# A decoder trunk on one core: u's tiles split in portions, merge factors spread together, roots spread later, two more final tiles beside VectorE

## The chip, the cores and the metric

The kernel runs on one core of a Trainium2 chip. The metric is the device time of one execution in microseconds (us). The time before is 2108.82 us, the median of three runs (2108.45 to 2113.14). The profile is one more execution of its own, which took 2107.84 us.

## The reference

A trunk of two layers over 1024 positions of width 1024, all in fp32. Each layer is a mixer and a dense MLP, both with RMS norm ahead and a residual add behind. The first mixer is a spatial gate, the second a dilated attention in three groups of heads. Cut to what matters:

```python
def rms_norm(x, g):
    return x * rsqrt(mean(x * x, -1) + EPS) * g

def chunk_gating_mixer(h, ...):                 # layer 0
    u, v = split(gelu(h @ w_in), 2)
    v = layer_norm(v, ln_g, ln_b)
    mixed = einsum('gts,bnsgc->bntgc', tril(w_s), v) + b_s
    return (u * mixed) @ w_out

def dilated_attention_mixer(h, ...):            # layer 1
    for g, (window, dil) in enumerate(((128, 1), (512, 4), (2048, 16))):
        num[g], den[g], m[g] = dilated_group(q[g], k[g], v[g], rel_bias)
    scale = [exp(m[g] - max(m)) for g in range(3)]
    return (sum(num * scale) / sum(den * scale)) @ w_out

for layer in range(2):
    h = h + mixer(rms_norm(h, mix_g))
    h = h + relu(rms_norm(h, mlp_g) @ w_up) ** 2 @ w_down
return rms_norm(h, final_g)
```

## The kernel before

**Layout and precision.** The residual stream h lies transposed in SBUF, 8 tiles of 128 features by 1024 positions. A half is 512 positions. Every fp32 product is made of three passes in a rounded fp32 type: an operand is split into hi, a copy that ScalarE makes (L226), and lo = x - hi, which VectorE makes (L227), and TensorE multiplies hi by hi, hi by lo and lo by hi into one bank (`mm`, L198). A tile of eight k is so 24 matmuls of 128x512.

**What sets the order.** TensorE's order is the order of the code. Beside the main line run generators on a modelled clock: `flow.add(gen, after)` puts one in the list, and the main line's `flow.pump()` advances those whose time has come; `yield ns` puts a generator off by that much modelled time. So a number in `flow.add` or `yield` says between which matmuls of the main line a generator's instructions stand. The other engines' orders follow from the same program by a scheduler that works with priorities; `tc.high_priority` lifts an instruction, `tc.issue_after(x)` keeps what stands in it behind the instruction x. Each engine then runs its own list strictly in that order.

**Banks.** The eight PSUM banks are two pools: three banks called mm and five called at. A product waits until the bank that its tile was given has been read out.

**Mixer 0.** `v` is made first, in three groups of chunks (`gi` 0, 1, 2) of up to six banks each. ScalarE's Gelus (L731) empty them, with 1/rms of the positions as scale. That root is found behind a group's last products (`sq[gi].rms`), and `spread_rms` (a generator) spreads it over 128 partitions: four transposes of `rs` on TensorE (L205, at<-ident,rs) and ScalarE's copy to `rsb`. The gate's weights give row sums by two matmuls a half (at<-wsh,tr and at<-wsl,tr), read by VectorE at L683. Then `u` is made: 16 tiles, eight m by two halves s, in groups of m (0, 1, 2), (3), (4), (5, 6, 7). `u_out` empties a tile: VectorE multiplies by `rsb` into a temp (L790), ScalarE takes the Gelu (L791), VectorE multiplies four chunks of v in place (L794). When a half's last tile is out, `u_split(s)` splits all eight m of it for the product with w_o: four hi copies (ScalarE) and four lo (VectorE, y<-vg,y) of 128x128 per m. Numbered in their order, tile 14 is (s = 1, m = 5), 15 is (1, 6), 16 is (1, 7). Beside that, `prepare` makes sums of w_qkv's blocks for a seven-product scheme, splits them (tr) and stores them by SyncE's queue (wd<-tr), which also carries the loads.

**Attention.** `merge(hp, i)` joins the three groups' results for a pair of heads hp and a half i. It makes factors f of 128x3x4x2, and for g = 1, 2 and then 0: `factors(g)` copies them out to 128x512 (ScalarE), `spread_factors` transposes that on TensorE into an at bank, and VectorE multiplies the numerators by it (L1694 for g = 1, 2). Between g's it yields modelled time, so that matmuls of the main line stand between.

**The end.** The last norm is done by `final` for a half and for the quarters 2 and 3 (columns 512 to 767 and 768 to 1023): the root (L256 to L265), its spread, then eight tiles h x g x pb by VectorE (L1878), stored in pairs of k by SyncE (outT<-t). In quarter 3 the pair k = 4, 5 goes another way (`ASIDE`): ScalarE copies pb (L1869) and makes h x g (L1875), GpSimd multiplies (L1876).

Of the kernel before, what the change touches and what calls it, by code (L numbers as in the profile page):

```python
# [31 lines left out]
def half(s):  # L32
    return slice(s * HALF, (s + 1) * HALF)


def blk(b, n=1):
    return slice(b * P, (b + n) * P)
# [80 lines left out]
BESIDE = (8, 9, 10)  # L118
STEPS = (5, 3)
ROOTS = ((0, 7, 0, 1, 0), (1, 7, 0, 1, 2))  # L120
GATE, ROWS, RB = 6, 10000, 5
NARROW = 68
ASIDE = {768: (4,)}
EARLY = 4
PACE = (1700.0, 1800.0, 3000.0)
LAT = dict(sum=2600.0, rms=2600.0, tile=1600.0, gate=8500.0, soft=5500.0, turn=4200.0, fe=1300.0, v=2000.0, qk=4200.0, merge=2600.0, out=700.0, fex=3.0, ve=1600.0, vd=6000.0, ex=18000.0, ones=900.0)
# [3 lines left out]
def trunk(ctx: ExitStack, tc: tile.TileContext, xT, w_u, w_v, w_o, w_s, b_s, w_qkv, w_vt, w_bo, rel,  # L130
# [524 lines left out]
    def spread_rms(s):  # L655
        pb = spread(rs[:, 4 * s:4 * s + 4])
        nc.scalar.activation(rsb[:, half(s)], pb, AF.Copy)
        yield 0
# [76 lines left out]
    for gi, chunks in enumerate(((0, 1, 2), (3, 4, 5), (6, 7))):  # L735
        banks = {}
        for k in range(KT):
# [35 lines left out]
            for e, i, n, f in order:  # L773
                x, c = ys[n // 4][k], blk(n % 4)
                matmul(banks[n, f], x[e == 1][:, c], w[e == 2][:, half(f)], start=(k == 0 and e == 0),
                       stop=(k == 7 and e == 2))
                if e == 2:
                    flow.pump()
                if (gi, k, i, f, e) in ROOTS:
                    for _ in sq[gi].sums():  # L780
                        pass
                    sq[gi].rms(rs[:, 4 * gi:4 * gi + 4])
                    flow.add(spread_rms(gi), 4000)
                if k == 7 and e == 2 and f == 1 and (i or gi == 2):
                    v_out(banks, chunks[:i + 1])

    def u_out(m, s, ps):
        t = temp()
        with tc.high_priority(offset=PRIO):
            nc.vector.tensor_tensor(t, ps, rsb[:, half(s)], op=ALU.mult)  # L790
        nc.scalar.activation(t, t, AF.Gelu)  # L791
        for b in range(4):
            x = vg[4 * s + b][:, blk(m)]
            nc.vector.tensor_tensor(x, x, t[:, blk(b)], op=ALU.mult)  # L794

    def u_split(s):
        out = []
        for m in range(8):
            hi, lo = pair().both()
            for b in range(4):  # L800
                split(hi[:, blk(b)], lo[:, blk(b)], vg[4 * s + b][:, blk(m)])
            out.append((hi, lo))
        return out

    us = []
    for tiles in ((0, 1, 2), (3,), (4,), (5, 6, 7)):
        w = [weight(w_u[m]) for m in tiles]
        if tiles[0] == 3:
            flow.add(prepare(PREPARED[0], PACE[0]))
        for s in range(2):  # L810
            for i, m in enumerate(tiles):
                b = mm_bank()
                mm(b, w[i], KCOLS, ys[s])
                flow.until(lambda: gated[4 * s + 3].t is not None)
                u_out(m, s, b)
            if tiles[-1] == 7:
                us.append(u_split(s))


    sq = [Square(half(0)), Square(half(1))]  # L820
# [821 lines left out]
    def merge(hp, i):  # L1642
# [38 lines left out]

        rest = None
        fe_ns = LAT["fe"] * (2.2 if hp == 3 else LAT["fex"])
        for g in (1, 2):
            fe = factors(g)
            if g == 2 and hp == 3:
                mine = factors(0)
            yield fe_ns
            if hp < 3:
                yield from turn_for(CALM[3])  # L1690
            pb = spread_factors(fe)
            t = temp()
            with tc.issue_after(whole[hp, 0]) if hp == 3 and (hp, 0) in whole else nullcontext():
                nc.vector.tensor_tensor(own(t, g), permuted(us_[g].N, i, g), own(pb, g), op=ALU.mult)  # L1694
            if rest is None:
                rest = t
            else:
                nc.vector.tensor_tensor(rest, rest, t, op=ALU.add)
# [258 lines left out]
```

## Time and profile before

| | us |
|---|---|
| median of 3 runs | 2108.82 |
| lowest, highest | 2108.45, 2113.14 |
| profiled execution | 2107.84 |
| its span | 2106.1 |
| outside the span | 1.74 |
| TensorE busy in the span | 2083.1 |

The granted TensorE clock is 0.998. The profile's page gives busy time by engine and the chain that ended last; the trace gives what each engine waited for, and rows of instructions in order of time. Such a row is: start, duration, engine, line, operation, output<-inputs, shapes, count, and in brackets the idle time before it with what ended it. Rows of several instructions merge neighbours of one kind, and neighbouring instructions overlap a little, so a pitch is a difference of starts rather than a duration.

### The profile page before, as it was taken

What the parts mean: (1) busy time and instruction counts of PE and PEld (TensorE: products, weight loads), DVE (VectorE), ACT (ScalarE), POOL (GpSimd) and SP (SyncE); (2) the same over time, 40 slices, a digit from 0 to 9 for tenths busy, and PEclk for the clock granted to TensorE, in tenths of its full rate; (3) what the DMA queues carried; (4) which work ended last, traced back from release to release, by engine and by line L of the source; (5) the groups of instructions that cost most, each with busy time, mean ns of one, the idle gap of its engine ahead of it and who ended that gap; (6) DMA issues with size and microseconds to landing.
All of it is one profiled execution on the core that took longest, in us unless ns stands there. A gap on an engine that the chain in (4) does not pass through costs nothing.

```text
span 2106.1 us, 30736 instructions
## 1 busy us (share of the span) xinstructions
PE 2083.1 (99%) x10160; PEld 1720.9 (82%) x10160; DVE 1572.8 (75%) x2902; ACT 1183.3 (56%) x2387; POOL 498.7 (24%) x368
## 2 busy tenths in 40 slices
PE   9999999999999999999999999999999999999998
PEld 7888888888888888888888788888888888888887
DVE  7878759766689998887746666757985446987776
ACT  7645435566675555435556666776556556544432
POOL 3000124323324333430000000002432222433244
PEclk9999999999999999999999999999999999999999
DMA  6428813688766767644865656482256443655432
GB/s 221 130 91 297 308 36 135 200 278 271 261 221 195 230 213 226 233 160 151 307 208 154 184 163 187 156 271 80 91 196 204 146 152 131 203 163 163 141 115 80
DMA packets 224756, 387.10 MB, mean 184 GB/s; under 512 B 39897, under 2 KB 67668, under 8 KB 224596
## 3 DMA queue, kind: packets, MB, share of 16 engines
q1 hardware_dynamic: 215456, 383.77, 55.4%
q10 hardware_dynamic: 9140, 1.36, 0.4%
q8 instruction: 80, 1.31, 0.3%
q14 instruction: 80, 0.66, 0.1%
HBM read 252.24 MB, written 132.81 MB: 183 GB/s over the span
## 4 chain that ended last, share of the span: by engine, by line
PE 84%; DVE 8%; DMA 2%; ACT 2%; issue 2%; POOL 1%; SPq 0%; DVEq 0%; POOLq 0%; ACTq 0%
PE mm L198 42%; PE at L198 40%; PE at L205 2%; DVE y L227 1%; DVE t L227 1%; DVE tr L227 1%; DMA t<-in_w_qkv 1%; DMA h<-in_xT 1%; DVE wp L227 0%; DVE q L1438 0%; DVE r L444 0%; DVE hx L227 0%; DMA r<-in_w_v 0%; POOL t L284 0%; DVE b L449 0%
## 5 line engine op out<-in xcount | busy, mean ns | idle before, releaser
L227 DVE TENSOR_TENSOR wp<-r,wp 128x512 fp32r<-128x512 f32 (+3 forms) x399 | 324.7, 819 | 124.4 <-ACT wp L226 122.1
L226 ACT ACTIVATE wp<-r 128x512 fp32r<-128x512 f32 (+3 forms) x399 | 236.2, 597 | 317.2 <-PE at L198 195.4
L198 PE MATMUL mm<-t,wp 128*128 128x512 f32 x1368 | 344.8, 395 | 0.0
L198 PE MATMUL at<-hx,wp 128*128 128x512 f32 x1452 | 341.0, 389 | 1.7 <-DVE h L1080 1.6
L198 PEld LDWEIGHTS at<-hx,wp 128*128 128x128 f32 x1452 | 272.1, 188 | 60.0 <-DVE h L1080 3.1
L198 PEld LDWEIGHTS mm<-t,wp 128*128 128x128 f32 x1368 | 250.7, 188 | 52.9 <-issue 0.7
L284 POOL TENSOR_TENSOR t<-t 128x512 f32<-128x512 f32 (+1 forms) x60 | 76.8, 1281 | 801.7 <-ACT t L279 799.7
L198 PE MATMUL at<-y,wp 128*128 128x512 f32 x1008 | 245.3, 389 | 0.0
L198 PE MATMUL mm<-hx,wp 128*128 128x512 f32 x984 | 234.3, 389 | 0.0
L198 PEld LDWEIGHTS at<-y,wp 128*128 128x128 f32 x1008 | 189.0, 188 | 39.6 <-issue 0.4
L198 PEld LDWEIGHTS mm<-hx,wp 128*128 128x128 f32 x984 | 184.5, 188 | 38.7 <-DVE hx L227 0.2
L198 PE MATMUL mm<-y,wp 128*128 128x512 f32 x816 | 209.8, 396 | 1.1 <-DVE y L227 0.6
L382 POOL TENSOR_TENSOR t<-r 128x512 f32<-128x512 f32 (+3 forms) x62 | 85.0, 1372 | 476.3 <-DMA r<-in_w_up 146.4
L198 PEld LDWEIGHTS mm<-y,wp 128*128 128x128 f32 x816 | 149.2, 188 | 33.0 <-DVE y L227 1.1
L227 DVE TENSOR_TENSOR hx<-t,hx 128x512 fp32r<-128x512 f32 x192 | 158.7, 831 | 6.1 <-ACT hx L226 5.6
L198 PE MATMUL mm<-y,whi 128*128 128x512 f32 x512 | 158.3, 390 | 1.1 <-DVE t L790 1.1
L198 PE MATMUL at<-t,wp 128*128 128x512 f32 x552 | 130.6, 389 | 0.0
L226 ACT ACTIVATE hx<-t 128x512 fp32r<-128x512 f32 x192 | 119.1, 628 | 19.9 <-DMA t<-hid 16.0
L384 POOL TENSOR_TENSOR r<-r 128x512 f32<-128x512 f32 (+3 forms) x62 | 90.5, 1459 | 165.4 <-DVE wp L227 151.9
L198 PEld LDWEIGHTS at<-t,wp 128*128 128x128 f32 x552 | 103.6, 188 | 21.5
L1080 DVE TENSOR_TENSOR h<-h,at 128x512 f32<-128x512 f32 x144 | 97.8, 680 | 27.6 <-PE at L198 27.1
L198 PEld LDWEIGHTS mm<-y,whi 128*128 128x128 f32 x512 | 95.5, 188 | 21.1 <-issue 1.5
(247 smaller groups left out, 3466.2 us busy)
## 6 DMA issues: line engine op xcount, KB each, us to landing
t<-hid SPq DMA_DIRECT2D x182, 256.0 KB, 4.3
wd<-tr SPq DMA_DIRECT2D x154, 256.0 KB, 3.1
wp<-wd SPq DMA_DIRECT2D x77, 512.0 KB, 4.2
hid<-t SPq DMA_DIRECT2D x140, 256.0 KB, 2.9
r<-in_w_up SPq DMA_DIRECT2D x120, 256.0 KB, 2.8
r<-in_w_dn SPq DMA_DIRECT2D x80, 256.0 KB, 2.7
hid<-b SPq DMA_DIRECT2D x56, 256.0 KB, 2.9
r<-in_w_v SPq DMA_DIRECT2D x48, 256.0 KB, 3.2
```

The lines of the kernel that those rows point to most:

```text
L198: nc.tensor.matmul(out, lhsT, rhs, **kw)
L205: nc.tensor.transpose(out, src, ident)
L226: return (nc.scalar.activation(hi, src, AF.Copy).ins, (engine or nc.vector).tensor_tensor(lo, src, hi.bitcast(F32), op=ALU.subtract).ins)
L227: (engine or nc.vector).tensor_tensor(lo, src, hi.bitcast(F32), op=ALU.subtract).ins)
L284: nc.gpsimd.tensor_tensor(self.acc, self.acc, sq, op=ALU.add)
L382: tt(r3, r[0, 0], r[1, 0], op=ALU.subtract)
L384: tt(r[1, 1], r[1, 0], r[0, 0], op=ALU.subtract)
L1080: return engine.tensor_tensor(hs[i, s], hs[i, s], src, op=ALU.add).ins
```

## The change

Four edits that have nothing to do with each other. Lines behind `u_out` move by four or five.

1. `spread_rms` joins the list with 10000 ns instead of 4000.
2. `u_split` takes a range of m. When s = 0's last tile is out, only m = 0 to 3 of `us[0]` are split; m = 4, 5 are split behind the emptying of tile 14 and m = 6, 7 behind that of tile 15. `us[1]` is split whole, as before.
3. In `merge`, for hp < 3 and i = 1, the factors of g = 2 are copied out ahead of those of g = 1, and the yield between g = 1 and g = 2 is 0. So g = 2's transposes stand behind fewer matmuls of the main line.
4. `ASIDE` has quarter 2 as well: its pair k = 4, 5 goes by ScalarE and GpSimd.

```diff
-GATE, ROWS, RB = 6, 10000, 5
+GATE, ROWS, RB, SPREAD = 6, 10000, 5, 10000
-ASIDE = {768: (4,)}
+ASIDE = {512: (4,), 768: (4,)}
...
-                    flow.add(spread_rms(gi), 4000)
+                    flow.add(spread_rms(gi), SPREAD)
...
     def u_out(m, s, ps):
         t = temp()
         with tc.high_priority(offset=PRIO):
-            nc.vector.tensor_tensor(t, ps, rsb[:, half(s)], op=ALU.mult)
+            emptied = nc.vector.tensor_tensor(t, ps, rsb[:, half(s)], op=ALU.mult).ins
...
+        return emptied
+
+    def u_split(s, ms=range(8)):
         out = []
-        for m in range(8):
+        for m in ms:
...
-                u_out(m, s, b)
+                emptied = u_out(m, s, b)
+                if tiles[-1] == 7 and s and i < 2:
+                    with tc.issue_after(emptied):
+                        us[0] += u_split(0, range(4 + 2 * i, 6 + 2 * i))
             if tiles[-1] == 7:
-                us.append(u_split(s))
+                us.append(u_split(s, range(4) if s == 0 else range(8)))
...
+        early = {2: factors(2)} if hp < 3 and i else {}
         for g in (1, 2):
-            fe = factors(g)
+            fe = early.pop(g, None) or factors(g)
...
-            yield fe_ns
+            yield 0 if g == 2 and hp < 3 and i else fe_ns
```

**TensorE behind the first group's last product.** at_581 to at_583 and mm_584 to mm_586 are the banks of the next group (gi = 1), at<-wsh and at<-wsl are the gate weights' row sums. Before:

```order
L198 MATMUL at_582<-wlo_564,y_223 128x512
L205 MATMUL at_621<-ident_82,rs_221 128x128 x4
L198 MATMUL at_583<-whi_565,y_505 128x512 x2
L198 MATMUL at_583<-wlo_564,y_505 128x512
L198 MATMUL at_630<-wsh_217,tr_460 128x512
L198 MATMUL at_630<-wsl_218,tr_460 128x512
L198 MATMUL mm_584<-whi_565,y_505 128x512 x2
L198 MATMUL mm_584<-wlo_564,y_505 128x512
L198 MATMUL mm_585<-whi_565,y_505 128x512 x2
L198 MATMUL mm_585<-wlo_564,y_505 128x512
L198 MATMUL at_643<-wsh_217,tr_460 128x512
```

Now:

```order
L198 MATMUL at_582<-wlo_564,y_223 128x512
L198 MATMUL at_583<-whi_565,y_505 128x512 x2
L198 MATMUL at_583<-wlo_564,y_505 128x512
L198 MATMUL mm_584<-whi_565,y_505 128x512 x2
L198 MATMUL mm_584<-wlo_564,y_505 128x512
L198 MATMUL at_627<-wsh_217,tr_460 128x512
L198 MATMUL at_627<-wsl_218,tr_460 128x512
L198 MATMUL mm_585<-whi_565,y_505 128x512 x2
L198 MATMUL mm_585<-wlo_564,y_505 128x512
L198 MATMUL mm_586<-whi_565,y_505 128x512 x2
L198 MATMUL mm_586<-wlo_564,y_505 128x512
```

The four transposes of rs have left this place (they stand behind the second product into mm_584, eleven rows on), the product into mm_584 comes ahead of the first row sums.

**VectorE at the end of u.** vg_1047 to vg_1400 are the chunks of s = 1, vg_549 to vg_1044 those of s = 0. mm_2273 is tile 14 before, mm_2237 tile 14 now, mm_2313 tile 15 now. Before, where tile 14 is emptied:

```order
L227 TENSOR_TENSOR y_2465<-vg_1391,y_2465 128x128
L227 TENSOR_TENSOR y_2465<-vg_1400,y_2465 128x128
L227 TENSOR_TENSOR wlo_2511<-r_2513,whi_2512 128x512
L227 TENSOR_TENSOR wlo_2511<-r_2517,whi_2512 128x512
L227 TENSOR_TENSOR tr_2319<-t_2109,tr_2318 128x512
L790 TENSOR_TENSOR t_2324<-mm_2273,rsb_220 128x512
L227 TENSOR_TENSOR tr_2342<-t_2310,tr_2341 128x512
L530 TENSOR_TENSOR t_2312<-t_2312,t_2314 128x512
L794 TENSOR_TENSOR vg_1047<-vg_1047,t_2324 128x128
L794 TENSOR_TENSOR vg_1084<-vg_1084,t_2324 128x128
L794 TENSOR_TENSOR vg_1391<-vg_1391,t_2324 128x128
```

Now, first where tile 14 is emptied, then where tile 15 is:

```order
L227 TENSOR_TENSOR y_2456<-vg_1400,y_2456 128x128
L227 TENSOR_TENSOR wlo_2511<-r_2513,whi_2512 128x512
L227 TENSOR_TENSOR wlo_2511<-r_2517,whi_2512 128x512
L227 TENSOR_TENSOR tr_2283<-t_2109,tr_2282 128x512
L790 TENSOR_TENSOR t_2288<-mm_2237,rsb_220 128x512
L227 TENSOR_TENSOR y_2295<-vg_549,y_2295 128x128
L227 TENSOR_TENSOR y_2295<-vg_552,y_2295 128x128
L227 TENSOR_TENSOR y_2295<-vg_561,y_2295 128x128
L227 TENSOR_TENSOR y_2295<-vg_1044,y_2295 128x128
L794 TENSOR_TENSOR vg_1047<-vg_1047,t_2288 128x128
```

```order
L227 TENSOR_TENSOR tr_2341<-t_2274,tr_2340 128x512
L790 TENSOR_TENSOR t_2352<-mm_2313,rsb_220 128x512
L227 TENSOR_TENSOR y_2359<-vg_549,y_2359 128x128
L227 TENSOR_TENSOR y_2359<-vg_552,y_2359 128x128
L227 TENSOR_TENSOR y_2359<-vg_561,y_2359 128x128
L227 TENSOR_TENSOR y_2359<-vg_1044,y_2359 128x128
L794 TENSOR_TENSOR vg_1047<-vg_1047,t_2352 128x128
L794 TENSOR_TENSOR vg_1084<-vg_1084,t_2352 128x128
L794 TENSOR_TENSOR vg_1391<-vg_1391,t_2352 128x128
L794 TENSOR_TENSOR vg_1400<-vg_1400,t_2352 128x128
L227 TENSOR_TENSOR y_2368<-vg_549,y_2368 128x128
L227 TENSOR_TENSOR y_2368<-vg_552,y_2368 128x128
```

Before, y_2465 (m = 4 of s = 1) and all of s = 0's splits stand ahead of tile 14's L790. Now s = 0's m = 4 (y_2295) stands behind it, and m = 6 (y_2359) and m = 7 (y_2368) behind tile 15's.

**TensorE in a merge (hp = 0, i = 1).** at_11674 and at_11676 hold g = 1's spread factors, at_11710 and at_11702 those of g = 2; mm_11501 and mm_11503 take the product of the main line. Before:

```order
L198 MATMUL mm_11439<-y_9290,wp_11220 128x512 x3
L205 MATMUL at_11674<-ident_82,t_11455 128x128 x4
L198 MATMUL mm_11501<-t7_9640,wp_11278 128x512 x3
L198 MATMUL mm_11501<-t7_9684,wp_11278 128x512 x3
L198 MATMUL mm_11501<-t7_9723,wp_11278 128x512 x3
L198 MATMUL mm_11501<-t7_9778,wp_11278 128x512 x3
L205 MATMUL at_11710<-ident_82,t_11681 128x128 x4
L198 MATMUL at_11721<-tr_11612,V_11581 128x256
```

Now:

```order
L198 MATMUL mm_11439<-y_9290,wp_11220 128x512 x3
L205 MATMUL at_11676<-ident_82,t_11457 128x128 x4
L198 MATMUL mm_11503<-t7_9640,wp_11278 128x512 x3
L198 MATMUL mm_11503<-t7_9684,wp_11278 128x512 x3
L205 MATMUL at_11702<-ident_82,t_11455 128x128 x4
L198 MATMUL mm_11503<-t7_9723,wp_11278 128x512 x3
L198 MATMUL mm_11503<-t7_9778,wp_11278 128x512 x3
L198 MATMUL at_11719<-tr_11614,V_11583 128x256
```

The transposes of g = 2 stand behind two of the four products with t7 instead of behind all four. VectorE's multiplication by at_11702 (L1699 now, L1694 before) keeps its place in VectorE's list, behind the sum with that product (L1443 before) and the split of N (L227).

More of the change, by code (lines that the diff above doesn't have):

```diff
@@ L794, in u_out @@
             nc.vector.tensor_tensor(x, x, t[:, blk(b)], op=ALU.mult)
-    def u_split(s):
+        return emptied
+    def u_split(s, ms=range(8)):
         out = []
-        for m in range(8):
+        for m in ms:
             hi, lo = pair().both()
```

## Prediction

> **What bounds the kernel now.** I read the page first: busy time by engine, then the chain that ended last.
>
> ```profile
> span 2106.1 us, 30736 instructions
> PE 2083.1 (99%) x10160; PEld 1720.9 (82%) x10160; DVE 1572.8 (75%) x2902; ACT 1183.3 (56%) x2387; POOL 498.7 (24%) x368
> PE 84%; DVE 8%; DMA 2%; ACT 2%; issue 2%; POOL 1%; SPq 0%; DVEq 0%; POOLq 0%; ACTq 0%
> ```
>
> TensorE is busy for 2083.1 of 2106.1 us, so everything that is not matmul time comes to 23.0 us, the start and the tail included. The change takes away no matmul and adds none, so it can only move these 23 us. The second view is what TensorE waited for (total us, times, longest us):
>
> ```profile
> PE at L205 <- DVE rq L265: 2.5, 2, 2.3
> PE at L198 <- DVE t L1694: 2.4, 3, 0.8
> PE at L205 <- ACT vg L731: 1.7, 1, 1.7
> PE mm L198 <- DVE t L790: 1.1, 1, 1.1
> PE at L198 <- DVE rb L683: 0.4, 1, 0.4
> ```
>
> Each of the four parts aims at one of these rows: the roots at L731 and L683 (2.1 us), the portions at L790 (1.1), the factors at L1694 (2.4), the final tiles at the tail behind L265. What all of that could give is 1.7 + 0.4 + 1.1 + 2.4 = 5.6 us on TensorE and something in the tail. About 0.3% (6.3 us) is what a measurement of this kernel can tell from no change, so nearly every outcome lies within it. I work with the profiled execution, 2107.84 us, which is 0.98 us under the median of the runs shown (2108.82), and add the sum to the median.
>
> **First roots spread later.** TensorE around 43 us, then ScalarE's Gelus there (start, duration, operation, count, idle time before):
>
> ```profile
> 43.10 0.62 PE L205 MATMUL at<-ident,rs 128*128 128x128 f32 x4 [1.70 <-ACT vg L731]
> 43.59 0.73 PE L198 MATMUL at<-whi,y 128*128 128x512 f32 x2
> ...
> 44.38 0.40 PE L198 MATMUL at<-wsh,tr 128*128 128x512 f32 x1
> ...
> 44.85 0.63 PE L198 MATMUL mm<-whi,y 128*128 128x512 f32 x2
> ...
> 46.77 0.47 PE L198 MATMUL at<-wsh,tr 128*128 128x512 f32 x1 [0.37 <-DVE rb L683]
> ...
> 47.99 0.63 PE L198 MATMUL at<-whi,y 128*128 128x512 f32 x2
> 42.27 1.84 ACT L731 ACTIVATE vg<-at,rs 128x512 f32<-128x512 f32 x3
> 43.99 1.85 ACT L731 ACTIVATE vg<-mm,rs 128x512 f32<-128x512 f32 x3
> ```
>
> The 1.70 us is not a wait for the roots' transposes as such: it is the wait for a PSUM bank, which the first Gelu empties (42.27 plus a third of 1.84 is 42.9, and TensorE starts 0.2 later). Taking the transposes out leaves that wait whole. Their 0.49 us (43.10 to 43.59) were filler between two Gelus. Now the next product starts at 43.10 and takes what it took (43.59 to 44.38, 0.79): 43.89. By the new order a product into an mm bank follows, which needs the fourth Gelu, 43.99 + 0.62 = 44.61, and 0.2 more: 44.8, a new wait of 0.9. From there come 0.68 for it, 0.47 for the gate weights' sums (44.38 to 44.85), two products at 0.68 and 0.47 again, without the 0.37 for L683, since another bank is free by then: 47.8, against 47.99. The transposes are still to be paid, 0.49: 48.3. I take **+0.3 us**, with ends of -0.4 (only the 0.37 goes) and +0.7 (the 0.37 stays too). The second group's transposes (gi = 1) find no idle time of TensorE there before and get 0.
>
> **u's tiles in portions.** VectorE and ScalarE before the wait at 210.23, and TensorE there:
>
> ```profile
> 208.71 0.39 PE L198 MATMUL mm<-y,wlo 128*128 128x512 f32 x1
> 210.23 0.70 PE L198 MATMUL mm<-y,whi 128*128 128x512 f32 x2 [1.13 <-DVE t L790]
> 199.10 0.90 DVE L794 TENSOR_TENSOR vg<-vg,t 128x128 f32<-128x128 f32 x4
> 199.91 2.51 DVE L227 TENSOR_TENSOR y<-vg,y 128x128 fp32r<-128x128 f32 x12
> ...
> 203.94 3.73 DVE L227 TENSOR_TENSOR y<-vg,y 128x128 fp32r<-128x128 f32 x18
> 207.58 1.30 DVE L227 TENSOR_TENSOR wlo<-r,whi 128x512 fp32r<-128x512 f32 x2
> 208.78 0.69 DVE L227 TENSOR_TENSOR tr<-t,tr 128x512 fp32r<-128x512 f32 x1
> 209.38 0.69 DVE L790 TENSOR_TENSOR t<-mm,rsb 128x512 f32<-128x512 f32 x1
> 199.49 3.11 ACT L226 ACTIVATE y<-vg 128x128 fp32r<-128x128 f32 x15 [0.42 <-DVE vg L794]
> 210.12 0.63 ACT L791 ACTIVATE t<-t 128x512 f32<-128x512 f32 x1 [0.97 <-DVE t L790]
> ```
>
> VectorE empties tile 14 (the second half's m = 5) only at 209.38, because some thirty splits of y stand ahead of it; TensorE ends tile 16 at 209.10 and needs that bank. Pitches from these rows: a split of 128x128 takes 0.207 (3.73 for 18), an op of 128x512 0.6 (207.58 to 208.78 for two), L794's four 0.81 (199.10 to 199.91).
>
> Now 16 splits stand there instead, those of us[1]'s m = 0 to 3, paced by ScalarE's copies: from 199.9 to about 203.5. With wlo behind ScalarE's whi to 205.05 and tr to 205.65, tile 14 is emptied at T = 205.7 to 206.0. The wait of 1.13 goes: TensorE starts the first w_o tile at 209.1.
>
> What is late next: that tile multiplies all eight m of us[0], and the lows of m = 6 and 7 now stand behind the emptying of tile 15. From T: L790 0.6, m = 4's four 0.83, then L794 once the Gelu of 0.63 is over, m = 5's four, tr, L530, L531, five splits, tr: T + 6.5, where tile 15 is emptied (212.2 to 212.5); then 0.6 and m = 6's four, to 213.7 to 214.0; L794's 0.81 and m = 7's four, to 215.3 to 215.6. TensorE wants a low at the second of three matmuls of an m, one every 0.68 (24 of 0.227 make a tile of 5.44): m = 6 at 213.4, m = 7 at 214.1. So it waits 0.3 to 0.6 for the first, which puts m = 7 at 214.4 to 214.7, and then 0.9 more: 1.2 to 1.5, less the 1.13 that went. On this I take **+0.4 us**; the ends are -1.1 (the lows come in time) and +2.8 (below, under the rivals). Who is queued behind: the other splits of us[1] and the prepared weights' tr, which have a tile of 5.44 before they are wanted.
>
> **Merge factors at once.** The three waits on L1694 are alike (0.80 to 0.81 each); the first of them, on TensorE, VectorE and ScalarE:
>
> ```profile
> 1171.75 3.02 PE L198 MATMUL mm<-t,wp 128*128 128x512 f32 x12
> 1174.60 0.60 PE L205 MATMUL at<-ident,t 128*128 128x128 f32 x4
> ...
> 1177.65 0.95 PE L198 MATMUL at<-k,q 64*128 64x128 f32 x11 [0.81 <-DVE t L1694]
> 1174.80 0.69 DVE L1443 TENSOR_TENSOR t<-t,mm 128x512 f32<-128x512 f32 x1 [1.64 <-PE mm L198]
> 1175.96 0.69 DVE L227 TENSOR_TENSOR tr<-N,tr 128x512 fp32r<-128x512 f32 x1 [0.47 <-ACT tr L226]
> 1176.57 1.02 DVE L1694 TENSOR_TENSOR t<-N,at 128x512 f32<-128x512 f32 x1
> 1175.30 0.63 ACT L226 ACTIVATE tr<-N 128x512 fp32r<-128x512 f32 x1 [1.01 <-PE at L205]
> ```
>
> The second score tile waits for its bank, which the spread factors of g = 2 hold until L1694 has read them at 1177.6. The transposes now come six matmuls earlier, about 1.4 us (half of 1171.75 to 1174.60). That does not make L1694 run 1.4 earlier: VectorE works in order, and its order is unchanged there. Ahead of L1694 still stand L1443, which waits for the twelve products (1174.8 as before, or 0.3 later with the transposes among them), and the split of N, which waits for ScalarE's tr. Only the 0.47 in front of that split can go: ScalarE waited 1.01 for the transposes, and no longer does. Against that, a reduction now runs behind L1709 and L1710, so ScalarE's q copy in front of tr is late by 0.7. I take 0.3 for each of three, **-0.9 us** (ends 0 and 0.8 each, so 0 and -2.4). The factors' second copy on ScalarE is only moved to the first one's place, with 1 us idle there.
>
> **Two more final tiles on ScalarE and GpSimd.** VectorE, ScalarE and GpSimd in the tail, and the DMA rate from 2095 to 2107 us in 40 slices of 0.3 us:
>
> ```profile
> 2097.74 4.66 DVE L1878 SCALAR_TENSOR_TENSOR t<-h,vec,at 128x512 f32<-128x512 f32 x11
> 2098.67 0.38 ACT L1869 ACTIVATE t<-at 128x256 f32<-128x256 f32 x1 [2.74 <-PE at L205]
> 2098.95 0.89 ACT L1875 ACTIVATE t<-h,vec 128x256 f32<-128x256 f32 x2
> 2099.53 1.41 POOL L1876 TENSOR_TENSOR t<-t 128x256 f32<-128x256 f32 x2 [5.90 <-ACT t L1875]
> GB/s 0 0 232 382 260 242 393 239 7 375 423 68 229 382 413 430 294 191 393 290 328 386 266 382 362 283 369 379 389 382 382 393 68 0 0 0 0 0 0 0
> ```
>
> Eleven ops of VectorE become nine behind the last root; 4.66 for ten of 128x256 and one of 128x512 is 0.39 per 128x256, so VectorE is done 0.78 earlier. The new copy on ScalarE (0.38, some 0.28 of it not overlapped) stands ahead of the last square, on which the root waits: +0.28. Net -0.5 where VectorE ends; but the last six slices of the stores run at 369 to 393 GB/s, near the most these slices show, with two thirds of a microsecond of dips before. So I take **-0.3 us** (ends -0.5 and +0.3). GpSimd's 1.41 lies in its idle 5.90 and costs nothing.
>
> [...]
>
> **The sum**: +0.3 + 0.4 - 0.9 - 0.3 = -0.5 us: 2107.3 for a profiled execution, **2108.3** as a median.
>
> **The rivals.** *All gaps close* (chance 0.12): L683's 0.4, L790's 1.1, L1694's 2.4 and the tail's 0.5 go, nothing comes: -4.4, so 2104.4. Against it speak the unchanged order on VectorE in the merge, and m = 6 and 7 behind tile 15.
>
> *The weights' loads decide, and the portions lose* (0.15): before, ScalarE's second tr after the splits waited for a load until 208.5:
>
> ```profile
> 208.51 0.63 ACT L226 ACTIVATE tr<-t 128x512 fp32r<-128x512 f32 x1 [0.98 <-DMA t<-in_w_qkv]
> ```
>
> That tr stands ahead of tile 14's Gelu. I take the load to come 3.8 earlier with the stores that it queues behind, at 204.7, since VectorE gives these their data that much sooner. If it lands at 208.5 all the same, the Gelu ends at 209.7, L794 at 210.6, and by the same chain of 0.83, 0.6, 0.6, 1.65 and 0.6 tile 15 is emptied at 214.8, m = 6's lows are there at 216.3 and m = 7's at 218.0: a wait of 3.9 for 1.13, +2.8. It decides from a landing of about 205.5 on. The sum is then 0.3 + 2.8 - 0.9 - 0.3 = +1.9: 2110.7, slower than before.
>
> *Gaps only move* (0.2): the merge gives 0, because the q copy is as late as the wait was long, and the tail gives 0: +0.7, 2109.5. *GpSimd sets the end* (0.05), from the point where its two ops end after VectorE's 2102.4 - 0.5; before, it ended at 2100.94, so it needs a copy that is 1 us late: +0.6 for -0.3, 2109.2. That leaves 0.48 for the forecast.
>
> **Range and chances.** The cases span 2104.4 to 2110.7; the bounds together reach from -4.4 to +3.8 (2104.4 to 2112.6), but the four parts are independent and rarely all at one end. Runs of before themselves lie 0.4 below to 4.3 above their median. I give 2105.2 to 2111.4, which leaves out most of the first rival. Faster by over 0.3% needs more than all gaps: 0.03. Slower by over 0.3% needs +6.3, twice the worst part: 0.04. Within: 0.93.
>
> **What would show it.** Right: a wait of about 1 us on the fourth Gelu near 44 us and none on L683; no wait on L790 near 209, but two on y's splits in the first w_o tile, 1.2 to 1.5 together; the waits on the merge's L1699 at 0.4 to 0.6 each; VectorE's end 0.5 closer to the last root's, and stores ending 0.3 earlier. Wrong: a w_o tile that runs through, waits on the merge gone or grown past 0.8, or TensorE waits of microseconds at a place that the change does not name.

## The result, and the profile after

The changed kernel takes 2113.62 us (median of 20 runs, 2108.84 to 2117.70) against 2109.11 us before (20 runs, 2106.31 to 2113.14): a ratio of 1.0021, interval 1.0015 to 1.0027, so 4.4 us slower (3.2 to 5.7). Forecast were -0.5 us and at most 2111.4. The profiled execution has a span of 2111.9 us, 5.8 more than before.

The page's head:

```profile
span 2111.9 us, 30752 instructions
PE 2085.4 (99%) x10160; PEld 1721.8 (82%) x10160; DVE 1579.0 (75%) x2900; ACT 1182.4 (56%) x2390; POOL 497.5 (24%) x370
```

What TensorE waited for, by the view of waits (total, times, longest):

```profile
PE mm L198 <- DVE y L227: 3.3, 3, 2.5
PE at L205 <- DVE rq L265: 3.0, 2, 2.8
PE at L198 <- DVE tr L227: 2.0, 4, 0.9
PE at L198 <- DVE t L1699: 2.0, 3, 0.7
PE at L198 <- ACT vg L731: 1.0, 1, 1.0
PE mm L198 <- ACT vg L731: 0.8, 1, 0.8
```

The waits on L790 and L683 are gone, as the change meant. In their place stand 3.3 us on the splits y (0.6 before), and 2.0 on tr (1.4 before). And TensorE is busy 2.3 us longer with the same 10160 matmuls: some of them ran slower, which the list of waits can't show.

To see where the time went I set the start of each matmul against that of the same matmul in before's trace; the difference is the lag. It is +0.7 at 140 us, +4.0 at 290, +4.8 at 850, +5.8 at 940, +5.1 at 1165, +5.9 at 1400, and +5.8 at the end. So 3.3 of 5.8 us are lost between 140 and 290 us. TensorE there, in the first w_o tile (start, duration, and in brackets the wait ahead of it):

```profile
213.74 0.39 PE L198 MATMUL mm<-y,whi 128*128 128x512 f32 x1
216.67 0.60 PE L198 MATMUL mm<-y,whi 128*128 128x512 f32 x1 [2.54 <-DVE y L227]
217.07 0.63 PE L198 MATMUL mm<-y,wlo 128*128 128x512 f32 x1
217.50 0.63 PE L198 MATMUL mm<-y,whi 128*128 128x512 f32 x1
218.28 0.80 PE L198 MATMUL mm<-y,whi 128*128 128x512 f32 x1 [0.16 <-DVE y L227]
218.88 0.63 PE L198 MATMUL mm<-y,wlo 128*128 128x512 f32 x1
```

The same place in stretches; the first number behind the last bracket is the granted clock:

```profile
214.00:216.70 2.70, 0.16 (x2) 0.03 (x1) 2.19 (x7) 1.63 (x3) 0.00 (x0) 1.00 0.52 203
216.70:218.00 1.30, 1.30 (x3) 0.59 (x3) 1.30 (x8) 1.09 (x5) 0.00 (x0) 0.58 0.56 214
218.00:219.00 1.00, 0.84 (x3) 0.62 (x3) 1.00 (x5) 0.34 (x1) 0.00 (x0) 0.50 0.00 0
...
221.00:224.00 3.00, 3.00 (x15) 2.47 (x14) 3.00 (x13) 1.92 (x6) 0.00 (x0) 1.00 0.95 358
```

TensorE runs through m = 0 to 5 and waits 2.54 for m = 6's lows. Then the matmuls stand 0.4 apart instead of 0.227, and longer ones hide the wait for m = 7: the clock is at 0.50 until 220.3. From the tile's start to there some 4.6 us are lost; less the 1.13 that before waited ahead of this tile, that is about the 3.3 by which this stage grew.

What came late on VectorE:

```profile
207.89 0.68 DVE L790 TENSOR_TENSOR t<-mm,rsb 128x512 f32<-128x512 f32 x1
...
214.51 0.69 DVE L227 TENSOR_TENSOR tr<-t,tr 128x512 fp32r<-128x512 f32 x1 [0.66 <-ACT tr L226]
215.12 0.68 DVE L790 TENSOR_TENSOR t<-mm,rsb 128x512 f32<-128x512 f32 x1
...
217.34 0.89 DVE L227 TENSOR_TENSOR y<-vg,y 128x128 fp32r<-128x128 f32 x4
```

On ScalarE:

```profile
213.33 0.64 ACT L226 ACTIVATE whi<-r 128x512 fp32r<-128x512 f32 x1 [2.43 <-DMA r<-in_w_o]
```

And on SyncE's queue (the end of the row has the number of DMAs):

```profile
202.93 1.92 SPq L187 DMA_DIRECT2D t<-in_w_qkv  x4
207.11 1.69 SPq L527 DMA_DIRECT2D wd<-tr  x3
208.85 1.54 SPq L187 DMA_DIRECT2D r<-in_w_o  x3
...
258.22 5.88 SPq L187 DMA_DIRECT2D r<-in_w_o  x6
```

Tile 14 is emptied at 207.89, tile 15 at 215.12, m = 7's lows end at 218.2. ScalarE stood 2.43 us at a copy of a w_o load, and VectorE's tr, which stands ahead of tile 15's L790, waited for ScalarE's tr behind that copy. SyncE issued this load at 208.85, behind four w_qkv loads and three stores. In before, whose SyncE queue follows, it stood ahead of them, and the last group of w_o loads came at 254.63 with five loads; now it has six, at 258.22:

```profile
198.74 0.56 SPq L187 DMA_DIRECT2D r<-in_w_o  x1
...
254.63 5.62 SPq L187 DMA_DIRECT2D r<-in_w_o  x5
```

The other three places on TensorE: the roots (two waits on Gelus), the merge (hp = 0), and the tail's root:

```profile
43.63 0.73 PE L198 MATMUL at<-whi,y 128*128 128x512 f32 x2 [0.97 <-ACT vg L731]
45.36 0.73 PE L198 MATMUL mm<-whi,y 128*128 128x512 f32 x2 [0.77 <-ACT vg L731]
...
1182.64 0.95 PE L198 MATMUL at<-k,q 64*128 64x128 f32 x11 [0.68 <-DVE t L1699]
...
1194.30 0.40 PE L198 MATMUL at<-tr,V 128*68 128x128 f32 x2 [0.61 <-DVE tr L227]
...
2104.22 0.40 PE L205 MATMUL at<-ident,rq 128*128 128x128 f32 x2 [2.81 <-DVE rq L265]
```

ScalarE in the merge:

```profile
1182.85 0.49 ACT L226 ACTIVATE tr<-at 128x384 fp32r<-128x384 f32 x1 [0.88 <-DMA od<-tr]
```

VectorE in the tail:

```profile
2103.99 3.87 DVE L1883 SCALAR_TENSOR_TENSOR t<-h,vec,at 128x512 f32<-128x512 f32 x9
```

And what the DMA engines moved from 2100.8 us on, in slices of 0.3:

```profile
GB/s 0 0 253 410 212 256 386 232 34 382 396 62 0 58 375 382 420 362 369 386 382 382 382 382 386 383 382 383 389 376 389 379 45 0 0 0 0 0 0 0
```

### The profile page after: what moved, and what is told of

Same layout as the page of the kernel before. It is cut to its first block, busy times and chain, and to the rows that moved or that the text cites. A ratio compares the mean times of both kernels' runs of the same rounds, so it can differ in the third digit from the quotient of the medians.

```text
span 2111.9 us, 30752 instructions
## 1 busy us (share of the span) xinstructions
PE 2085.4 (99%) x10160; PEld 1721.8 (82%) x10160; DVE 1579.0 (75%) x2900; ACT 1182.4 (56%) x2390; POOL 497.5 (24%) x370
## 4 chain that ended last, share of the span: by engine, by line
PE 86%; DVE 7%; DMA 3%; ACT 2%; issue 1%; POOL 0%; SPq 0%; DVEq 0%; ACTq 0%; POOLq 0%
PE mm L198 44%; PE at L198 41%; PE at L205 2%; DVE y L227 1%; DMA r<-in_w_v 1%; DVE tr L227 1%; DMA h<-in_xT 0%; DMA t<-in_w_qkv 0%; DVE hx L227 0%; DMA t<-hid_(0, 0)_6227 0%; DVE wp L227 0%; DMA r<-in_w_vt 0%; DVE r L444 0%; DVE q L1442 0%; DVE wlo L227 0%
## 5 line engine op out<-in xcount | busy, mean ns | idle before, releaser
L227 DVE TENSOR_TENSOR wp<-r,wp 128x512 fp32r<-128x512 f32 (+3 forms) x399 | 325.3, 820 | 124.5 <-ACT wp L226 121.7
L227 DVE TENSOR_TENSOR hx<-t,hx 128x512 fp32r<-128x512 f32 x192 | 161.4, 845 | 6.4 <-ACT hx L226 6.4
```

The costliest lines, as they stand in the source:

```text
L227: (engine or nc.vector).tensor_tensor(lo, src, hi.bitcast(F32), op=ALU.subtract).ins)
```

## The experiments

A trace is one execution, and one execution of the same program can lag another by more than a part of this change is worth. `aside` has before's program up to the tail, and lags it by -1.1 us at 60 us. So each kernel is read twice: by its timed runs (11 against 33 of before on the same chip, an interval of some 1.9 us to each side), and by what its trace lost against before's in each stage (us):

| kernel | timed ratio (interval) | 0 to 140 | 140 to 290 | 850 to 940 | 1165 to 1400 |
|---|---|---|---|---|---|
| the change | 1.0021 (1.0015 to 1.0027) | +0.7 | +3.3 | +1.0 | +0.8 |
| after_again | 1.0016 (1.0007 to 1.0025) | +1.1 | +2.2 | +0.5 | +0.5 |
| portions | 1.0002 (0.9993 to 1.0011) | -0.2 | +2.5 | +0.3 | +0.3 |
| portions_again | 1.0007 (0.9998 to 1.0016) | +1.7 | +3.4 | +2.3 | +0.1 |
| spread_portions | 1.0009 (1.0000 to 1.0018) | +0.3 | +3.0 | +0.5 | -0.4 |
| filled | 1.0004 (0.9995 to 1.0013) | +1.0 | +0.8 | +0.7 | +0.4 |
| load_first | 1.0003 (0.9995 to 1.0012) | +0.3 | +2.9 | +0.2 | -0.3 |
| early67 | 1.0018 (1.0009 to 1.0027) | -0.2 | +4.2 | +0.3 | +0.1 |
| after_act | 1.0013 (1.0004 to 1.0022) | +1.3 | +0.8 | +2.1 | 0.0 |
| early67_act | 0.9989 (0.9980 to 0.9998) | +1.0 | 0.0 | +0.7 | -0.8 |
| before_act | 1.0003 (0.9994 to 1.0012) | +0.2 | +0.5 | +2.9 | -0.7 |
| no_portions | 1.0006 (0.9997 to 1.0015) | +1.2 | +0.2 | +1.2 | +0.6 |
| spread | 0.9999 (0.9990 to 1.0009) | +1.0 | +0.5 | 0.0 | +0.3 |
| merge | 1.0001 (0.9992 to 1.0010) | +0.7 | -0.2 | +1.1 | +1.2 |
| aside | 0.9994 (0.9985 to 1.0003) | -1.1 | +0.1 | +0.5 | +0.5 |
| whole67_act | 1.0013 (1.0004 to 1.0021) | +0.3 | +0.4 | +4.2 | +0.5 |
| best | 0.9989 (0.9980 to 0.9998) | -0.2 | -0.7 | +0.8 | -0.7 |

The first column is almost all scatter: without the roots' edit the lag at 140 us is the lateness of ScalarE's first Gelu (42.27 in before) to within 0.02 us, whatever the kernel, and with it 0.11 to 0.14 more.

**portions and portions_again**: the edits of `u_out`, `u_split` and the loop alone.

> The portions of u alone, the other three parts left as before. Theory A (the portions cost nearly all of the 4.5 us: the first w_o tile waits for the lows of m = 6 and 7, which stand behind tile 15's emptying, ScalarE's copy of a late w_o load holds that up, and the granted clock is halved for some 3.5 us after the wait): +3.0 to +4.5 us, a wait of 2 to 3 us on y's splits near 214 us, and a granted clock near 0.5 behind it. Theory B (the portions cost only the wait's face value above the 1.13 that they remove, the rest comes from the roots' place and from later stages): +0.5 to +1.6 us, and a clock that stays at 1.00.

> The portions alone once more. Their trace showed 2.5 us lost at the first w_o tile, their timed runs +0.4 (interval 1.9 to each side). Theory D (a stable loss of 2 to 3 us): the timed runs of both together at +1 to +2.5. Rival (the loss is in some executions only): again within 0.7 of before.

Timed at 1.0002 and 1.0007, near theory B; the traces lose 2.5 and 3.4 us between 140 and 290 us, near theory A. In the first, TensorE waited 1.04 and 0.65, about what the prediction had (0.3 to 0.6, then 0.9), and the clock halved none the less; in the second it waited 1.89 and 0.64, the clock stayed at 1.00, and 1.12 went at a w_o weight near 263 us. Every one of the five traces with these portions loses 2.2 to 3.4 us there, and none of the four without portions that keep SyncE's loads loses more than 0.5. The loss in the traces is stable, then, but the timed runs of the portions alone show less of it: the two together lie at +1.0 (1.3 to each side).

**filled**: the portions, and small matmuls in the wait.

```diff
-                mm(b, w[i], KCOLS, us[s])
+                if m or s:
+                    mm(b, w[i], KCOLS, us[s])
+                else:
+                    mm(b, w[i], KCOLS, us[s], range(6))
+                    keep = at_bank()
+                    for _ in range(FILL):
+                        nc.tensor.matmul(keep[:, 0:P], ones, ones, start=True, stop=True)
+                    mm(b, w[i], KCOLS, us[s], (6, 7))
```

> The portions alone, with ten small matmuls of ones by ones (twenty passes, some 2.2 us, into a bank that nobody reads) put into the first w_o tile ahead of m = 6, so that TensorE is busy while it waits. Theory A: the lows come no earlier, but the clock stays at 1.00 behind the wait, so the time is 1.3 to 2 us below the portions alone. Theory B (the clock has no part in it): the same as the portions alone within 0.5 us.

The matmuls of ones cover the wait on TensorE:

```profile
214.06 2.39 PE L838 MATMUL at<-ones 128*128 128x128 f32 x20
216.21 0.71 PE L199 MATMUL mm<-y,whi 128*128 128x512 f32 x2
```

And the tile goes on at a granted clock of 1.00, the first number behind the last bracket:

```profile
216.00:220.00 4.00, 4.00 (x22) 3.37 (x21) 4.00 (x12) 1.83 (x6) 0.00 (x0) 1.00 0.42 160
```

The trace loses 0.8 where the portions alone lost 2.5 and 3.4. The timed runs (1.0004) don't tell it from them: the fill takes its 2.2 us (214.06 to 216.21) whether TensorE would have waited that long or not, and where the wait is shorter that is more than it saves. Nor does this trace test the clock: the lows of m = 6 ended at 215.24 here, some 1.0 us after TensorE would have wanted them, and whether a wait of that length would have halved the clock at this place is not shown. That the clock costs something is read from the other traces (matmuls 0.4 apart for 0.227); what it costs on average is not shown.

**load_first**: the portions, with the one load that ScalarE waited for issued by ScalarE's own queue, where it lands before it is wanted.

```diff
+            split(hi[:, half(i)], lo[:, half(i)], load(src[:, half(i)], own and own(), nc.scalar if side and i else None))
-        w = [weight(w_o[m]) for m in tiles]
+        w = [weight(w_o[m], side=tiles == (2,)) for m in tiles]
```

> The portions alone, with one load moved: the second half of the third w_o weight (the one that ScalarE waited 2.43 us for) is issued from ScalarE's queue, ahead of the splits. Theory A: VectorE's wait of 0.66 ahead of tile 15's emptying goes, the wait at the first w_o tile shrinks by 0.6 to 1.0 us; if it gets below about 2 us the clock stays at 1.00 too, so 1 to 2.5 us below the portions alone, which still leaves +0.5 to +2.5 against before. Rival: the load is not what held tile 15 up, and the time is that of the portions alone within 0.5 us.

A miss for theory A: the waits were 1.76 and 0.66, and 0.77 came at a w_o weight at 262 us. The load did hold tile 15 up: without it 6.48 us pass from tile 14's emptying to tile 15's, for 6.79 to 7.50 in the five traces with it. But in this execution VectorE was 1.1 late for TensorE from tile 12 on, behind loads of w_qkv, so the wait stayed as long, and the next one came at the next late load. The 2 us below which theory A had the clock stay at 1.00 was the author's estimate, and no run shows such a bound: the clock halved behind 1.04 and 0.65 in portions.

**early67**: the portions cut otherwise.

```diff
-                if tiles[-1] == 7 and s and i < 2:
+                if tiles[-1] == 7 and s and i == 0:
                     with tc.issue_after(emptied):
-                        us[0] += u_split(0, range(4 + 2 * i, 6 + 2 * i))
+                        us[0] += u_split(0, range(6, 8))
-                us.append(u_split(s, range(4) if s == 0 else range(8)))
+                us.append(u_split(s, range(6) if s == 0 else range(8)))
```

> Portions cut otherwise: m = 0 to 5 of us[0] at once, m = 6 and 7 behind tile 14's emptying; nothing behind tile 15's. Theory A: the lows of m = 6 and 7 are there in time, the w_o load keeps its old place in SyncE's queue, so the wait at the first w_o tile is under 0.5 us, the clock stays at 1.00 and the time is 0 to 1.3 us below before. Theory B (VectorE simply has too much to do there, whatever the order): still a wait of 1 us or more and +0.5 to +1.6 us.

Neither theory had this: 1.0018, slower. In the first two w_o tiles only 0.22 of waiting is left (on tile 15's bank), and the loss stands 45 us later. TensorE there:

```profile
259.07 1.22 PE L198 MATMUL mm<-y,whi 128*128 128x512 f32 x2 [3.45 <-ACT whi L226]
260.10 0.63 PE L198 MATMUL mm<-y,wlo 128*128 128x512 f32 x1
```

ScalarE:

```profile
258.39 0.63 ACT L226 ACTIVATE whi<-r 128x512 fp32r<-128x512 f32 x1 [4.16 <-DMA r<-in_w_o]
```

SyncE's queue:

```profile
254.08 8.39 SPq L187 DMA_DIRECT2D r<-in_w_o  x7
```

SyncE's last group has seven w_o loads now, behind sixteen stores of the prepared weights, and TensorE, which came 1.1 us earlier than in before, waits 3.45 for the first of them, with matmuls 0.42 apart behind it (260.10 to 260.52) for 0.227. From this came theory F: the portions lose by the w_o loads that they push behind those stores.

**early67_act, after_act and before_act**: those portions, the whole change, and before, each with all w_o loads on ScalarE's queue.

```diff
-            split(hi[:, half(i)], lo[:, half(i)], load(src[:, half(i)], own and own()))
+            split(hi[:, half(i)], lo[:, half(i)], load(src[:, half(i)], own and own(), queue))
-        w = [weight(w_o[m]) for m in tiles]
+        w = [weight(w_o[m], queue=nc.scalar) for m in tiles]
```

> Portions cut with m = 6 and 7 behind tile 14, and the w_o loads issued by ScalarE's queue. Theory F: the wait of 3.45 us near 259 us on ScalarE's copy of a w_o load goes, and none is left at 214 us: 3.5 us or more below the same portions with SyncE's loads (which were +3.8), so -1.2 to +0.3 against before. Rival (the loads take as long on any queue, since the DMA engines are 0.8 to 0.9 busy there): a wait of 2 us or more stays at 259 us and +2 or more against before.

> The whole change, with the loads of all w_o weights issued by ScalarE's queue instead of SyncE's, where they stand behind the prepared weights' stores. Theory F (what the portions cost is the w_o loads that they push behind those stores: first the one that ScalarE waits 2.43 us for, then the last six at 258 us, where TensorE wants them): 1.5 to 3.5 us below the whole change, so +1 to +3 against before. Rival (only VectorE's order counts, the lows of m = 6 and 7 stay late): within 0.7 us of the whole change, +3.7 to +5.

> The control: the kernel before with the w_o loads issued by ScalarE's queue. Theory F: nothing waits for these loads in before at full length, so within 1 us of before. If the queue alone changes the time, this shows by how much, and the two kernels above are read against it.

The queue alone does nothing to before that can be told (1.0003). With it early67 goes from 1.0018 to 0.9989 (2.3 us below before, where 1.2 was the most that was forecast), its trace from 4.2 lost to 0.0, with no wait at 259; 0.75 on tile 15's bank at 216.6 is what it still waits there. For early67 theory F is shown, in time and trace. For the whole change it is shown by the traces alone: 0.8 is lost there instead of 3.3 and 2.2, while the time, 1.0013, can't be told from 1.0021 and 1.0016, so by time the rival stands. What is left in that trace are the lows of m = 6 and 7, 0.94 and 0.65, the prediction's own wait, at a clock of 1.00; tile 15 is emptied 6.44 us behind tile 14, where the prediction worked out 6.5. The first of them, on TensorE:

```profile
215.61 0.50 PE L198 MATMUL mm<-y,whi 128*128 128x512 f32 x1 [0.94 <-DVE y L227]
```

**spread, merge, aside, no_portions, spread_portions**: the other parts alone and together. The first three are one edit of before each:

```diff
 spread
-                    flow.add(spread_rms(gi), 4000)
+                    flow.add(spread_rms(gi), SPREAD)
 merge
+        early = {2: factors(2)} if hp < 3 and i else {}
-            fe = factors(g)
+            fe = early.pop(g, None) or factors(g)
-            yield fe_ns
+            yield 0 if g == 2 and hp < 3 and i else fe_ns
 aside
-ASIDE = {768: (4,)}
+ASIDE = {512: (4,), 768: (4,)}
```

with SPREAD = 10000. no_portions is the change without the portions, spread_portions has the portions and the roots alone:

```diff
 no_portions, against the change
-                if tiles[-1] == 7 and s and i < 2:
-                    with tc.issue_after(emptied):
-                        us[0] += u_split(0, range(4 + 2 * i, 6 + 2 * i))
-                us.append(u_split(s, range(4) if s == 0 else range(8)))
+                us.append(u_split(s))
 spread_portions, against portions
-                    flow.add(spread_rms(gi), 4000)
+                    flow.add(spread_rms(gi), SPREAD)
```

> The roots' spread alone. By the steps of the prediction +0.3 us, a wait of 0.8 to 1.0 on the fourth Gelu, none on L683. Theory A: +0.3 to +0.8. Theory C: +1.5 to +3, with a later wait grown beyond that at 43 us.

> The merge factors alone. By the trace of the changed kernel the waits on L1699 went from 0.80 to 0.67 each and the waits on the values' turned tiles behind them grew by 0.1 to 0.7 each, so -0.4 to +0.8 us in all. Theory A: within 0.8 us of before. Theory C: up to +1.5.

> The two more final tiles alone. By the trace of the changed kernel the last root is 0.46 us later (a wait of 2.81 for 2.35) and VectorE has 0.78 less behind it: -0.5 to +0.3 us. Up to the tail its program is that of before, so its profile also shows how far two executions of one program lie apart.

> The change without the portions (roots later, merge factors at once, two more final tiles). Theory A (the portions bear most of the change's cost, through the wait at the first w_o tile and the halved clock; alone they were hidden by the luck of loads): within 1.5 us of before, no wait above 1.2 us near 210, clock at 1.00. Theory C (the other three parts cost most, foremost the roots spread later, which put everything behind 43 us late against the loads): +2.5 to +4.5 us.

> The roots' spread and the portions together, merge and final tiles as before. Theory D (the parts simply add up, each being lost in the scatter when alone; by the traces the roots cost 0.2 us and the portions 2.4 to 3.4): +2 to +3.5 us. Theory E (the two together are worse than their sum, since TensorE is late at 43 us and the first w_o tile then falls on a worse phase of the loads): +4 to +5. If neither part costs anything: within 1 us.

None alone can be told from before; no_portions and spread_portions lie at +1.3 and +1.9 us (1.9 to each side). Theory C (+2.5 to +4.5 for no_portions) is unlikely by that and has nothing in the traces, though the wait near 210 us is 1.30 in no_portions, a little over theory A's bound of 1.2. Theory D's lower end (+2 for spread_portions) is nearest, and theory E falls. The two timings of the whole change together lie 2.8 us (2.2 to each side) above no_portions, which fits what the traces lose by the portions. spread shows 0.84 and 0.77 on Gelus and none on L683. merge shows its price in the trace: the waits on L1695 (before's L1694) are 0.68, 0.68 and 0.67, but those on tr behind them 0.64, 0.37 and 0.87. The six traces with the merge edit lose 0.6 on average from 1165 to 1400 us, the eleven without it -0.1.

**after_again, whole67_act and best**: the whole change again; the whole change with early67's cut and ScalarE's loads; and early67_act with the two more final tiles.

```diff
 whole67_act, against the change (and early67_act's edit)
-                if tiles[-1] == 7 and s and i < 2:
+                if tiles[-1] == 7 and s and i == 0:
-                        us[0] += u_split(0, range(4 + 2 * i, 6 + 2 * i))
+                        us[0] += u_split(0, range(6, 8))
-                us.append(u_split(s, range(4) if s == 0 else range(8)))
+                us.append(u_split(s, range(6) if s == 0 else range(8)))
 best, against early67_act
-ASIDE = {768: (4,)}
+ASIDE = {512: (4,), 768: (4,)}
```

> The whole change once more, beside the kernels below on the same chip: +3.2 to +5.7 us against before as measured first, and by its second trace the wait on m = 6 and 7 in the first w_o tile again, 1.7 us or more. [...]

> The whole change with two things mended: m = 6 and 7 of us[0] behind tile 14 instead of tile 15, and the w_o loads by ScalarE's queue. Theory F: the 3 to 3.5 us of the first w_o tile go, what is left is 0.2 for the roots, 0.6 for the merge, -0.1 for the final tiles and some -1 to -2 for the portions: -1.5 to +0.5 against before. Rival (roots and merge cost more in company): +1 to +3.

> Only the parts that did not lose: portions cut with m = 6 and 7 behind tile 14, w_o loads by ScalarE's queue, two more final tiles aside. Theory F: -2 to -3 us against before.

after_again waited 1.70 and 0.66 at the first w_o tile with the clock at 1.00, and lost 2.2. best, at 0.9989 (1.84 us below before by the medians), is as fast as early67_act: the final tiles add nothing that can be told. whole67_act missed: its trace loses only 0.4 between 140 and 290, as theory F wants, but 4.2 near 890 us, where TensorE waits for a ScalarE evacuation of the first MLP:

```profile
889.87 4.52 PE L198 MATMUL mm<-hx,wp 128*128 128x512 f32 x12 [2.04 <-ACT mm L1107]
```

The clock drops again behind it, to 0.69 in the mean of four us:

```profile
892.00:896.00 4.00, 4.00 (x14) 3.21 (x13) 3.93 (x9) 0.54 (x1) 0.70 (x1) 0.69 1.01 357
```

before_act loses 2.9 at that place too, the others 0.0 to 2.3, with the same instructions: it looks like scatter of this kernel. But the five kernels with ScalarE's loads lose 2.1 there on average and the twelve others 0.7, so a share of that edit is not excluded. A least-squares fit of twelve timed ratios (all but filled, load_first, early67, after_act and before_act) to a sum of parts, weighted by their intervals, gives +1.3 (1.0 to each side) for the portions, +1.1 (1.3) for the roots, +1.8 (1.4) for the merge, -0.4 (1.3) for the final tiles and -1.3 (1.3) for early67's portions with ScalarE's loads; whole67_act lies 1.5 above it.

## Why the prediction was wrong, point by point

**The portions** (forecast +0.4): this is the step that failed. Its mechanism was right: the 1.13 on L790 went, and the first w_o tile waits twice for the lows of m = 6 and 7. Its size was not: five traces lose 2.2 to 3.4 us there. Three things add up.

First, "T + 6.5, where tile 15 is emptied" is T + 7.2 in the trace (207.89 to 215.12), and 6.8 to 7.5 in the four other traces with these portions, because ScalarE stands at a w_o load. The step counted VectorE's list and ScalarE's, and of SyncE's only the w_qkv loads, which indeed hold ScalarE up no more. It did not follow what these pass: the w_o load. The rival on "the weights' loads" had the right place and the wrong load. With that load on ScalarE's queue it is T + 6.4 (after_act) and T + 6.5 (load_first).

Second, T itself is 207.9 where TensorE ends tile 16 at 209.8, so 1.9 ahead instead of the 3.1 to 3.4 forecast (2.5 to 3.0 in the four others). VectorE's tr ahead of tile 12 stands behind ScalarE's, which waits for w_qkv loads in both traces; here the wait ends 1.8 later, where TensorE is 0.7 later. Before, then now:

```profile
190.71 0.63 ACT L226 ACTIVATE tr<-t 128x512 fp32r<-128x512 f32 x1 [4.30 <-DMA t<-in_w_qkv]
...
192.52 0.63 ACT L226 ACTIVATE tr<-t 128x512 fp32r<-128x512 f32 x1 [4.37 <-DMA t<-in_w_qkv]
```

That is ill luck of this execution: VectorE's lateness at tile 12 against TensorE's lies between -0.5 and +1.2 over all traces, and spread and before_act, without portions, have +0.6 and +0.5.

Third, a wait was priced at its own length, and TensorE's clock behind it was not thought of: 3.41 us at a clock of 0.50 cost 1.7 us, by reckoning. The first trace of the portions shows this alone: it waits 1.04 and 0.65, together 1.7 for the 1.2 to 1.5 forecast, and loses 2.5. Where the clock stayed at 1.00 (after_again, portions_again), TensorE came to the w_o weights near 260 us earlier and lost 0.7 and 1.7 there, so the two prices stand in for each other. With the clock the prediction's premise fails that the change "can only move these 23 us": TensorE's busy time itself grew by 2.3.

**The roots** (forecast +0.3): +0.1, and right in its steps. 0.77 on the fourth Gelu for 0.9 forecast, L683's 0.37 gone, transposes of 0.3 paid behind: less the first Gelu's lateness (0.62 in this execution, ahead of the edit), TensorE is 0.18 early where 47.99 stood before (forecast 0.2) and 0.11 late behind the transposes.

**The merge** (forecast -0.9, ends 0 and -2.4): wrong in sign. The waits on L1699 shrank from 0.81 to 0.68, by 0.13 instead of 0.3. The range ended at 0 since nothing was named that could come behind; what came is the wait on tr for the values, from 0.16, 0.17 and 0.21 to 0.61, 0.30 and 0.88. The first two belong to the edit: 0.47 to 0.66 and 0.21 to 0.38 in the six traces that have it, at most 0.25 in the others. The third is 0.81 to 0.89 in all six, but 0.64 to 0.90 in three of the others too. ScalarE's copy at 1182.85 waits 0.88 for a store of the split N (od<-tr) before it may use that temp again, and such waits stand in all six traces with the edit and in none without: with g = 2's factors made early, one more temp is held, and the ring of temps comes round to a tile still being stored. That the held temp is the cause is argued from the buffer rotation; that the merge edit costs some 0.6 there is shown by the traces.

**The final tiles** (forecast -0.3): 0.0. VectorE's nine ops take 3.87 for 4.66, as forecast; the root came 0.46 late instead of 0.28 (2.81 for 2.35), and from there the end is 7.68 us away instead of 8.12. The 0.46 is not the copy on ScalarE, whose L256 follows TensorE at once in both traces. It is two small ops of VectorE in the root that take 0.39 and 0.37 for 0.15, beside GpSimd's op of quarter 2 (2102.18 to 2103.59). Before, then now:

```profile
2096.75 0.15 DVE L262 TENSOR_TENSOR ra<-rr,rv 128x2 f32<-128x2 f32 x1
...
2102.53 0.39 DVE L262 TENSOR_TENSOR ra<-rr,rv 128x2 f32<-128x2 f32 x1
2103.24 0.37 DVE L263 SCALAR_TENSOR_TENSOR ra<-ra,rr 128x2 f32<-128x2 f32 x1
```

So GpSimd's pace did not set the end, as that rival had it: GpSimd's last two ops end at 2106.98, VectorE's nine at 2107.86. No run shows the +0.6 of that rival; it was the author's estimate, two ops at 0.31, the 0.70 of GpSimd's 1.41 for two in before less VectorE's 0.39. What the runs showed in its place are the two small ops, 0.46 longer together beside GpSimd's op, about what the change gave behind the root (0.44). That GpSimd's op is the cause is the author's reading. From 2105.0 to 2110.4 the stores run at 362 to 420 GB/s, close to the most that these slices show, and the author reads the stores as the bound there, as the prediction did.

Summed by the traces: 0.1 + 2.7 + 0.6 + 0.0 = +3.4 us, where 2.7 is the mean of the five traces with these portions (2.5, 3.4, 3.0, 3.3, 2.2) less the 0.2 that four without lose; timed +4.4 (3.2 to 5.7). Of the 3.9 between that sum and the forecast of -0.5, the portions make 2.3 and the merge 1.5. Open stays why the portions alone were timed at +0.4 and +1.5 us with 2.5 and 3.4 in their traces, and how often the clock halves in executions without a profile.

**The rivals and the range**: "all gaps close" was far off. The slower rival, 2110.7, came nearest: its +2.8 for the portions is close to the 2.7 found, but it had this from another load and without the clock, and it kept the merge's -0.9. The prediction took 0.3% to be the least that runs can tell; twenty runs of each kernel told 0.21%.

## What to carry to other kernels

When an edit lets an engine's list run earlier, follow every queue that this list feeds: here stores and other loads came to stand ahead of the next weights' loads in SyncE's list, and the wait came back at the next place that needs those weights, twice (2.54 us near 214 us in the change, 3.45 near 259 in early67), until the loads had a queue of their own. Behind one wait of 2.54 us (the change), and behind two of 1.04 and 0.65 (portions), TensorE ran 3.41 us at a clock of 0.50; behind 1.89 and 0.64 (portions_again) it did not. So a wait like these is priced with 1.7 us more at the upper end, an estimate from the 3.41 at 0.50. Where an op is moved to an idle engine, look at the small ops of another beside it: two of VectorE's took 0.39 and 0.37 us beside GpSimd's op, for 0.15. And where parts are worth less than the scatter of the start, read them in one stage of many traces rather than in the total.

## What the runs showed of the hardware

In five of the eighteen traces TensorE's granted clock fell to 0.50 before the tail, each time once and for 3.41 us: from 216.92 (the change), 216.24 (portions), 217.49 (spread_portions), 258.56 (early67) and 891.05 us (whole67_act). In the 3.41 us just before, TensorE stood idle for 2.54, 1.69, 1.83, 2.93 and 2.03 us. Two waits of 1.04 and 0.65 were followed by the half clock (portions, the first two rows); 1.70 and 0.66 were not (after_again, the last two):

```profile
212.83:216.24 3.41, 1.72 (x7) 0.85 (x6) 3.41 (x14) 2.06 (x6) 0.00 (x0) 1.00 0.60 231
216.24:219.65 3.41, 3.41 (x10) 2.63 (x9) 3.41 (x8) 1.26 (x2) 0.00 (x0) 0.50 0.70 272
...
212.08:215.49 3.41, 2.40 (x11) 1.66 (x9) 2.88 (x9) 1.82 (x4) 0.00 (x0) 1.00 0.60 231
215.49:218.90 3.41, 2.07 (x8) 1.43 (x9) 3.41 (x15) 1.92 (x6) 0.00 (x0) 1.00 0.47 179
```

Nor were 1.76 and 0.66 (load_first) and 1.89 and 0.64 (portions_again), where the clock stayed at 1.00. The change and the portions each have the half clock in one of two traces, and the length of the waits alone does not tell which: it came behind 1.69 in all (portions) and not behind 2.53 (portions_again). What decides is not shown.

VectorE's L262 of 128x2 took 0.15 us in the tail where GpSimd ran nothing beside it (before, at 2096.75), and 0.38 to 0.39 where it did (before at 2090.71; the change at 2096.50 and 2102.53).

ScalarE's queue took the sixteen w_o loads at no cost that could be told (before_act, 1.0003), while on SyncE's they stood behind up to sixteen stores, and early67 went from 1.0018 to 0.9989 by it. No run here measures bandwidth by queue; what the runs show is the wait of 3.45 us at 259 us in early67, which is gone in early67_act.
